# Moving the sums of w_down from the attention stage into the first MLP product of a two-layer f32 trunk

## The chip, the cores and the metric

The kernel runs on one core of a Trainium2 chip (trn2). The metric is the device time of one execution in microseconds (us), lower is better. The kernel before was timed three times: 2888.29, 2884.75 and 2887.67 us, median 2887.67.

The core has a matrix engine (PE, TensorE; PEld is its weight load), a vector engine (DVE, VectorE), a scalar engine (ACT, ScalarE), a general engine (POOL, GpSimd), and SP (SyncE), which here only issues DMA transfers. Each engine runs its own instructions strictly in the order in which they stand; an instruction that waits holds up everything behind it on its engine.

## The reference, cut to what matters

Two layers over 1088 tokens (1024 of a prompt, 64 of a sample), width 1024. Each layer is a mixer (layer 0: pooling and a recurrence, layer 1: windowed attention), then cross-attention into 256 memory tokens, then an MLP. All is f32. What the change touches is the MLP and the stage ahead of it:

```python
x = x + cross_attn(rmsnorm(x, p['norm_cross'][layer]), mem_k[layer], mem_v[layer],
                   p['w_mq'][layer], p['w_mo'][layer])
x = x + sq_relu_mlp(rmsnorm(x, p['norm_mlp'][layer]), p['w_up'][layer], p['w_down'][layer])
...
def sq_relu_mlp(h, w_up, w_down):        # w_up 1024 x 4096, w_down 4096 x 1024
    return jnp.square(jax.nn.relu(h @ w_up)) @ w_down
```

## The kernel before, in words

**Precision.** A f32 product is made of three matmuls: each operand is split into a rounded part (made by ACT) and the remainder (a subtraction on DVE), and low x high, high x low and high x high are added up in PSUM (`split`, L234, and `product`, L216). So every weight tile costs an ACT and a DVE instruction before PE can use it.

**Tokens** lie in two halves, s=0 (512) and s=1 (576); `x` holds the residual stream, features on partitions.

**The MLP by seven products.** Both MLP products are cut into 2 x 2 blocks and made with seven block products where eight are usual, with sums and differences of blocks as operands (the Strassen-Winograd scheme).
- The token operands B11, B12, B21, B22, T1 to T4 of a half are made by `operands` (L959): DVE scales x by the norm and gain (`scaled`), subtracts, and splits. For s=0 this runs under the last projection of cross-attention (`project_back`), for s=1 in one piece at slot 5 of the first MLP product (`hook`, L1192).
- The weight operands of w_up (A11, A12, A22, S1 to S4) are made per *stream*, which is 256 of the 4096 columns of w_up: two loads of 512 KB into `st` tiles by SP, four sums of 128x512 on POOL (L1050 to L1054, in `Up.weights`, L1036), seven splits (ACT L236, DVE L239 into `wp`).
- The first product, `Up.run` (L1077), runs 32 *rounds* of seven products (*slots*) each; a round is one stream with one token half, a product is 12 matmuls of 256 (s=0) or 288 (s=1) columns. Streams are mostly used for two rounds, s=0 and then s=1. The list of streams is 0, 1, 0, 2, 3, ..., 15, 14: streams 0 and 14 are loaded and made twice and used for one round each time. The numbers 5 and 7 in `self.at` say how many slots ahead of its use a weight operand may be made; it also has to wait until the operand of the stream before is used up.
- At the end of a round `finish` (L1094) takes relu and square of the result u on ACT, four sums of u on POOL (L1103 to L1106) into two single tiles `ss` and `sq`, and queues three stores to HBM, which SP issues at the fifth slot of the next round.
- The second product (`mlp_down`, L1218) loads quarters of w_down, or sums of its quarters, and the stored u and its sums.

**The sums of w_down** are made ahead of the MLP, under cross-attention: `weights_sums` (L937), called twice per head at L929, so 16 times per layer. Each call loads 1 MB of w_down into one tile `quarters` with two DMAs (SP, L942), makes four sums of 128x512 on POOL (L948) and stores the 1 MB with one DMA (SP, L949). The tile is single, so the next load waits for the store before it.

**Order.** A scheduler places most instructions; `keep_in_program_order` and `manual_schedule` pin some engines to the order of the program. In cross-attention the DMAs and POOL sums of `weights_sums` are pinned in that way; in the first MLP product SP, POOL and PE are. POOL also makes rc (the power -0.5 of the norm, L322) and the sum o (L908) in cross-attention, and issues the loads of keys and values (L792, L795).

Of the kernel before, what the change touches and what calls it, by code (L numbers as in the profile page):

```python
# [46 lines left out]
def body(ctx, tc, I, O):  # L47
# [7 lines left out]
    def f32(ap):  # L55
        return ap.bitcast(F32)
# [159 lines left out]
    def product(ps, small, big):  # L216
        terms = small + big
        for i, (a, b) in enumerate(terms):
            pe.matmul(ps, a, b, start=i == 0, stop=i == len(terms) - 1)  # L219
# [559 lines left out]
    def cross(l, s, norm, p, then):  # L779
# [135 lines left out]
        for j in range(4):  # L915
# [12 lines left out]
            for q in range(2):  # L928
                weights_sums(l, 8 * s + 2 * j + q, p)  # L929
# [6 lines left out]

    def weights_sums(l, q, p):  # L937

        a = p.tile([128, 4, 512], F32, tag="quarters", name="quarters", bufs=1)
        keep = tc.keep_in_program_order  # L940
        for i in range(2):
            keep(nc.sync.dma_start(a[:, 2 * i:2 * i + 2],  # L942
                                   I["w_down"][l][256 * q + 128 * i:256 * q + 128 * i + 128]
                                   .rearrange("p (h n) -> p h n", h=2)))

        for to, one, two, op in ((3, 1, 3, OP.add), (1, 0, 1, OP.subtract), (0, 3, 0, OP.subtract),
                                 (2, 2, 0, OP.subtract)):
            keep(pool.tensor_tensor(a[:, to], a[:, one], a[:, two], op))  # L948
        keep(nc.sync.dma_start(sums[l][q // 2][:, :, q % 2], a))  # L949
# [9 lines left out]
    def operands(s, g, nm, raw, ops, alloc):  # L959
# [14 lines left out]
        scaled(raw["B11"], 0, 0)  # L974
        yield
# [3 lines left out]
        parts("B11")  # L979
# [3 lines left out]
        scaled(raw["B21"], 4, 0)  # L983
        yield
        pool.tensor_tensor(raw["T3"], raw["B22"], raw["B12"], OP.subtract)
        dve.tensor_tensor(raw["T2"], raw["B22"], raw["T1"], OP.subtract)
        parts("T2")
        yield
        dve.tensor_tensor(raw["T4"], raw["T2"], raw["B21"], OP.subtract)
        for b in ("B21", "T1", "T4", "B22", "T3"):  # L990
            parts(b)
            yield
# [5 lines left out]
    class Up:  # L998


        def __init__(self, l):
            self.l = l
            self.streams = [0, 1, 0] + list(range(2, 16)) + [14]
            self.rounds = [(0, 0), (1, 0), (1, 1), (2, 1)]
            for k in range(3, 17):
                self.rounds += [(k, 0), (k, 1)] if self.streams[k] != 14 else [(k, 0)]
            self.rounds.append((17, 1))
# [14 lines left out]
            for w in range(count):  # L1022
                wanted = min(first[v] for v in range(w, min(w + 7, count))) - 5
# [12 lines left out]
        def weights(self, w):  # L1036
# [18 lines left out]
            elif name == "S3":  # L1055
                self.load(k + 1, 0)
                if k + 1 == len(self.streams):
                    W.resume(self.l, 2)
                    W.ahead()
# [17 lines left out]
        def run(self, ops, bufs, us, hook):  # L1077
# [16 lines left out]
            def finish(r):  # L1094
# [10 lines left out]
                pool.tensor_tensor(t[1], u[:, 2], t[0], OP.subtract)  # L1105
                pool.tensor_tensor(t[3], t[1], u[:, 1], OP.subtract)  # L1106
# [5 lines left out]
            store, sums_of_u = [], []  # L1112
            for i, (r, m) in enumerate(self.slots):
# [5 lines left out]
                cs.setdefault(r, bufs[r % 3])  # L1119
# [11 lines left out]
                product(ps, small, big)  # L1131
# [10 lines left out]
    def mlp(l, back, nm, last):  # L1142
# [18 lines left out]
        with phase(f"mlp{l}") as outer:  # L1161
# [29 lines left out]

            def hook(i):  # L1192
                r, m = up.slots[i]
# [6 lines left out]
                if r + 1 == len(up.rounds) and i % 7 == 0:  # L1200
# [522 lines left out]
```

## Time and profile before

| | |
|---|---|
| median of three runs | 2887.67 us |
| the profiled execution | 2890.01 us |
| its span, first to last instruction | 2888.2 us |
| PE busy | 2680.4 us (93%) |
| DVE / ACT / POOL busy | 1693.6 / 1247.5 / 772.2 us |
| cross-attention, layer 0 and 1 | 420 to 696 us, 1825 to 2110 us |
| first MLP product, layer 0 and 1 | 732 to 1113 us, 2147 to 2525 us |
| second MLP product, layer 0 and 1 | 1113 to 1454 us, 2525 to 2870 us |

PE is busy nearly all the time, so the time is the matmuls, the stretches in which PE stands still, and the stretches in which its granted clock is at the lower of its two levels (1.2 instead of 2.4 GHz, 0.5 in the records). A row of a timeline gives start, duration, engine, line, instruction, and in brackets how long the engine had been idle before it and what ended that.

### The profile page before, as it was taken

Reading aid. Unit: us, or ns where it says so; the run is one execution under the profiler, and the core shown is the slowest. Engines: PE = TensorE matmul, PEld = TensorE weight load, DVE = VectorE, ACT = ScalarE, POOL = GpSimd, SP = SyncE. Lnnn points to the kernel's source line nnn. Section 1 sums busy time; section 2 is a strip of 40 time slices with the busy share of each in tenths; the row PEclk is TensorE's granted clock in tenths of the full one; section 3 lists DMA queues with packets and bytes.
Section 4 is the critical chain, followed back from the end, with each engine's and each line's share of the span. In section 5 each row is a group of like instructions: output and inputs, shape, how many; then the busy total and the mean of one; then the engine's idle time right before and its main releaser. Section 6 shows DMA issues by size and latency. Waiting matters only on the chain. (4 is left out here: it accounts for less than half of the span.)

```text
span 2888.2 us, 47649 instructions
## 1 busy us (share of the span) xinstructions
PE 2680.4 (93%) x19048; PEld 2547.6 (88%) x19048; DVE 1693.6 (59%) x2844; ACT 1247.5 (43%) x2113; POOL 772.2 (27%) x762
## 2 busy tenths in 40 slices
PE   8999998878799999999999999987788999899998
PEld 7978997777799999999988899867688999899998
DVE  5595766556755556555458467655486545555454
ACT  5584644233434434333337356333334444433334
POOL 3200013333465552000003013243435555500000
PEclk9999999999899999999999999999899999999999
DMA  8722245654244447555340321456433444575552
GB/s 267 221 73 81 66 118 192 198 172 153 60 150 135 151 131 264 194 181 181 98 93 23 94 59 53 150 179 204 161 95 111 151 143 126 171 247 181 181 181 78
DMA packets 403938, 416.30 MB, mean 144 GB/s; under 512 B 48528, under 2 KB 335264, under 8 KB 403716
## 3 DMA queue, kind: packets, MB, share of 16 engines
q1 hardware_dynamic: 394820, 386.20, 42.1%
q0 software_dynamic: 8896, 27.06, 3.0%
q8 instruction: 149, 2.44, 0.4%
q14 instruction: 73, 0.60, 0.1%
HBM read 303.94 MB, written 109.39 MB: 143 GB/s over the span
## 5 line engine op out<-in xcount | busy, mean ns | idle before, releaser
L219 PE MATMUL mm<-hpH,wp 128*128 128x288 f32 (+3 forms) x3008 | 731.8, 330 | 42.4 <-DVE q L821 27.6
L219 PEld LDWEIGHTS mm<-hpH,wp 128*128 128x128 f32 x3008 | 518.8, 190 | 86.3 <-DVE q L821 29.8
L219 PE MATMUL mm<-hpL,wp 128*128 128x288 f32 (+3 forms) x1504 | 473.4, 330 | 2.3 <-DVE hpL L297 2.2
L185 ACT ACTIVATE wp<-st 128x1024 fp32r<-128x1024 f32 x218 | 229.5, 1056 | 361.0 <-PE mm L219 222.2
L239 DVE TENSOR_TENSOR wp<-st,wp 128x512 fp32r<-128x512 f32 x252 | 215.9, 865 | 251.4 <-ACT wp L236 249.3
L219 PE MATMUL s<-T,wp 128*128 128x288 f32 (+1 forms) x2304 | 312.5, 294 | 37.0 <-DVE wp L239 36.7
L186 DVE TENSOR_TENSOR wp<-st,wp 128x1024 fp32r<-128x1024 f32 x218 | 273.0, 1254 | 120.4 <-ACT wp L185 119.7
L219 PEld LDWEIGHTS s<-T,wp 128*128 128x128 f32 x2304 | 301.2, 193 | 42.5 <-DVE wp L239 42.0
L219 PEld LDWEIGHTS mm<-hpL,wp 128*128 128x128 f32 x1504 | 288.8, 192 | 21.4 <-DVE hpL L297 3.2
L948 POOL TENSOR_TENSOR quarters<-quarters 128x512 f32<-128x512 f32 x128 | 182.0, 1422 | 347.6 <-DMA quarters<-in_w_down_dram 340.2
L236 ACT ACTIVATE wp<-st 128x512 fp32r<-128x512 f32 x252 | 144.6, 621 | 267.1 <-POOL st L1052 208.4
L322 POOL TENSOR_TENSOR rc<-rc,mhalf 128x4 f32<-128x4 f32 (+1 forms) x21 | 22.4, 1076 | 850.4 <-DVE rc L321 850.4
L185 ACT ACTIVATE wd<-st 128x1024 fp32r<-128x1024 f32 x70 | 73.7, 1055 | 313.3 <-PE t L1259 299.9
L219 PE MATMUL mm<-B,wp 128*128 128x256 f32 (+1 forms) x1536 | 204.6, 288 | 4.1 <-DVE wp L239 4.1
L219 PEld LDWEIGHTS mm<-B,wp 128*128 128x128 f32 x1536 | 197.2, 188 | 5.3 <-DVE wp L239 5.3
L186 DVE TENSOR_TENSOR wd<-st,wd 128x1024 fp32r<-128x1024 f32 x70 | 86.3, 1236 | 158.7 <-ACT wd L185 158.7
L1257 PE MATMUL s<-uhl,wd 128*128 128x256 f32 x560 | 156.7, 284 | 9.5 <-ACT uhl L236 9.5
L1258 PE MATMUL s<-uhl,wd 128*128 128x256 f32 x560 | 157.4, 282 | 0.0
L1259 PE MATMUL s<-uhl,wd 128*128 128x256 f32 x560 | 156.9, 281 | 0.0
L239 DVE TENSOR_TENSOR uhl<-ur,uhl 128x1088 fp32r<-128x1088 f32 x112 | 143.9, 1286 | 17.8 <-ACT uhl L236 17.6
L236 ACT ACTIVATE uhl<-ur 128x1088 fp32r<-128x1088 f32 x112 | 123.4, 1104 | 49.0 <-DMA ur<-u 47.1
L1081 DVE TENSOR_TENSOR uC<-s,uC 128x256 f32<-128x256 f32 (+1 forms) x320 | 133.5, 432 | 11.6 <-PE s L219 5.0
(402 smaller groups left out, 6269.7 us busy)
## 6 DMA issues: line engine op xcount, KB each, us to landing
ur<-u SPq DMA_DIRECT2D x112, 544.0 KB, 6.0
st<-in_w_up_dram SPq DMA_DIRECT2D x72, 512.0 KB, 4.7
quarters<-in_w_down_dram SPq DMA_DIRECT2D x64, 512.0 KB, 4.7
sums<-quarters SPq DMA_DIRECT2D x32, 1024.0 KB, 5.7
st<-sums SPq DMA_DIRECT2D x64, 512.0 KB, 5.8
st<-in_w_down_dram SPq DMA_DIRECT2D x48, 512.0 KB, 5.0
st<-in_w_mq_dram SPq DMA_DIRECT2D x32, 512.0 KB, 4.5
st<-in_w_mo_dram SPq DMA_DIRECT2D x32, 512.0 KB, 6.9
```

What stands on the lines that cost most here:

```text
L185: act.activation(wt[:, 0], st, AF.Copy)
L186: dve.tensor_tensor(wt[:, 1], st, f32(wt[:, 0]), OP.subtract)
L219: pe.matmul(ps, a, b, start=i == 0, stop=i == len(terms) - 1)
L236: act.activation(h, src, AF.Copy)
L239: dve.tensor_tensor(l, src, f32(h), OP.subtract)
L322: pool.tensor_tensor(rc[:m, b0:b1], rc[:m, b0:b1], mhalf[:m, b0:b1], OP.pow)
L948: keep(pool.tensor_tensor(a[:, to], a[:, one], a[:, two], op))
L1081: dve.tensor_tensor(to, b, a, op)
L1257: pe.matmul(ps, wl, uh, start=first, stop=False)
L1258: pe.matmul(ps, wh, ul, start=False, stop=False)
L1259: pe.matmul(ps, wh, uh, start=False, stop=half == 1 and g == 3 and k == 1)
```

## The change

Four things are changed.
1. `weights_sums` leaves cross-attention and becomes a part of `Up.run`. There it handles 32 *pieces* per layer, half as large as before (256 of 512 columns), one per six slots from slot 24 on: two loads at turn 0, four POOL sums of 128x256 at turn 3, two stores at turn 5. All pieces use the same two tiles.
2. Two of the four sums of u go from POOL to DVE.
3. `operands` yields in smaller steps and in another order. For s=1 one step runs per slot from slot 5 on, instead of all at slot 5. The remainders of B22 and T3 are subtracted on POOL instead of DVE, for both halves.
4. The streams are 15, 0, 1, ..., 15 (17 instead of 18 are made; only the first and the last round use a stream alone), a weight operand may be made nine slots ahead instead of five, the matmuls of the very first product are pinned, and the pool of the second product opens one round earlier.

```diff
-            for q in range(2):
-                weights_sums(l, 8 * s + 2 * j + q, p)
...
-        def parts(b):
+        def parts(b, engine=dve):
             if b not in ops:
                 ops[b] = alloc(b)
-            split(ops[b][:, 0], ops[b][:, 1], raw[b])
+            act.activation(ops[b][:, 0], raw[b], AF.Copy)
+            engine.tensor_tensor(ops[b][:, 1], raw[b], f32(ops[b][:, 0]), OP.subtract)
...
-        for b in ("B21", "T1", "T4", "B22", "T3"):
-            parts(b)
-            yield
+        yield
+        parts("T4")
+        yield
+        parts("B22", pool)
+        parts("T3", pool)
...
-            self.streams = [0, 1, 0] + list(range(2, 16)) + [14]
...
+            self.streams = [15] + list(range(16))
+            self.rounds = [(0, 0)] + [(k, s) for k in range(1, 16) for s in range(2)] + [(16, 1)]
...
-                wanted = min(first[v] for v in range(w, min(w + 7, count))) - 5
+                wanted = min(first[v] for v in range(w, min(w + 7, count))) - 9
...
-                pool.tensor_tensor(t[1], u[:, 2], t[0], OP.subtract)
-                pool.tensor_tensor(t[3], t[1], u[:, 1], OP.subtract)
+                dve.tensor_tensor(t[1], u[:, 2], t[0], OP.subtract)
+                dve.tensor_tensor(t[3], t[1], u[:, 1], OP.subtract)
...
+            def weights_sums(i):
+
+                piece, turn = divmod(i, 6)
+                if i < 0 or piece >= 32:
+                    return
+                q, at = piece // 2, slice(256 * (piece % 2), 256 * (piece % 2) + 256)
+                if not quarters:
+                    quarters.extend(nrm.tile([128, NT2], F32, tag="rb", name="quarters", bufs=2)[:, :512]
+                                    .rearrange("p (h n) -> p h n", h=2) for _ in range(2))
+                (a11, a21), (a12, a22) = ((t[:, 0], t[:, 1]) for t in quarters)
+                if turn == 0:
+                    for j, t in enumerate(quarters):
+                        rows = I["w_down"][self.l][256 * q + 128 * j:256 * q + 128 * j + 128]
+                        nc.sync.dma_start(t, rows.rearrange("p (h n) -> p h n", h=2)[:, :, at])
+                elif turn == 3:
+                    pool.tensor_tensor(a22, a21, a22, OP.add)
+                    pool.tensor_tensor(a21, a11, a21, OP.subtract)
+                    pool.tensor_tensor(a11, a22, a11, OP.subtract)
+                    pool.tensor_tensor(a12, a12, a11, OP.subtract)
+                elif turn == 5:
+
+                    for j, t in enumerate(quarters):
+                        nc.sync.dma_start(sums[self.l][q // 2][:, 2 * j:2 * j + 2, q % 2, at], t)
...
+                weights_sums(i - 24)
...
-                    for _ in operands(1, g, nm1, raw1, ops[1], operand):
-                        pass
...
+                if 5 <= i < 24:
+                    next(make1, None)
```

On POOL, in the second token half of cross-attention of layer 0, these rows stand before the change (kvst are keys and values on their way in, o is a sum that the attention result waits for):

```order
L795 DMA kvst<-in_cache_mem_v_dram 128x2x256
L948 TENSOR_TENSOR quarters<-quarters 128x512 x4
L795 DMA kvst<-in_cache_mem_k_dram 128x2x256
L948 TENSOR_TENSOR quarters<-quarters 128x512 x4
L908 TENSOR_TENSOR o_5613<-o_5613 128x2x64
```

At the same place after the change:

```order
L797 DMA kvst<-in_cache_mem_v_dram 128x2x256
L797 DMA kvst<-in_cache_mem_k_dram 128x2x256
L910 TENSOR_TENSOR o_5533<-o_5533 128x2x64
L794 DMA kvst<-v_2_704 128x512
L794 DMA kvst<-kT_3_801 128x512
```

The sums of quarters are gone from between the loads and ahead of o.

On SP, in the middle of the first MLP product of layer 0, this stands before (u, ss and sq are the stores of one round, st the loads of w_up):

```order
L1122 DMA u_5_6354<-uC_6361 128x3x256
L1122 DMA u_5_6354<-ss 128x2x256
L1122 DMA u_5_6354<-sq 128x2x256
L1033 DMA st<-in_w_up_dram 128x8x128 x2
L1122 DMA u_5_6354<-uC 128x3x288
L1122 DMA u_5_6354<-ss 128x2x288
L1122 DMA u_5_6354<-sq 128x2x288
```

And this after:

```order
L1140 DMA u_5_6226<-uC_6233 128x3x256
L1140 DMA u_5_6226<-ss 128x2x256
L1140 DMA u_5_6226<-sq 128x2x256
L1025 DMA st<-in_w_up_dram 128x8x128 x2
L1130 DMA sums_5_89<-quarters 128x2x256 x2
L1121 DMA quarters<-in_w_down_dram 128x2x256 x2
L1140 DMA u_5_6226<-uC 128x3x288
L1140 DMA u_5_6226<-ss 128x2x288
L1140 DMA u_5_6226<-sq 128x2x288
```

The two stores of a piece and, directly behind them, the two loads of the next piece have come in; the stores wait for POOL's sums, the loads for the landing of the stores.

On DVE, where the token operands of s=1 of layer 0 are finished, this stands before (T and B are remainders of operands, rc and ra unsplit ones, wp a weight operand, uC the rounds' own sums):

```order
L986 TENSOR_TENSOR rc<-rb,rc 128x1152
L1081 TENSOR_TENSOR uC<-s,uC 128x256
L989 TENSOR_TENSOR ra<-rc,rb 128x1152
L239 TENSOR_TENSOR T_6904<-rc,T_6904 128x1152
L239 TENSOR_TENSOR B_6906<-rb,B_6906 128x1152
L239 TENSOR_TENSOR T_6905<-rc,T_6905 128x1152
L1090 TENSOR_TENSOR uC<-uC,t 128x256
L239 TENSOR_TENSOR wp<-st,wp 128x512
```

And this after:

```order
L975 TENSOR_TENSOR rc<-rb,rc 128x1152
L1074 TENSOR_TENSOR uC<-s,uC 128x256 x2
L1083 TENSOR_TENSOR uC<-uC,t 128x256
L1074 TENSOR_TENSOR uC<-s,uC 128x256
L959 TENSOR_TENSOR T_6780<-rc,T_6780 128x1152
L959 TENSOR_TENSOR T_6781<-rc,T_6781 128x1152
L982 TENSOR_TENSOR ra<-rc,rb 128x1152
L1098 TENSOR_TENSOR ss<-uC,ss 128x256
```

More of the rounds' own sums now stand between the operands, two of them (L1098, L1099) new on DVE.

## Rows read from the trace of the kernel before

**Rows 1.** The page's busy times of the whole span.
```profile
PE 2680.4 (93%) x19048; PEld 2547.6 (88%) x19048; DVE 1693.6 (59%) x2844; ACT 1247.5 (43%) x2113; POOL 772.2 (27%) x762
```
**Rows 2.** Stretches us: PE, PEld, DVE, ACT, POOL busy (count), clock, DMA share, GB/s.
```profile
420.00:696.00 276.00, 229.87 (x1336) 203.45 (x1335) 159.63 (x259) 100.28 (x210) 104.72 (x88) 0.93 0.57 183
732.40:1112.90 380.50, 349.08 (x2706) 345.08 (x2704) 213.64 (x382) 160.09 (x233) 209.96 (x196) 0.97 0.43 134
1825.00:2110.00 285.00, 235.55 (x1356) 207.63 (x1354) 162.35 (x261) 100.18 (x211) 105.80 (x88) 0.93 0.56 179
2146.60:2525.00 378.40, 351.20 (x2705) 347.22 (x2703) 214.96 (x382) 160.22 (x233) 206.25 (x196) 0.97 0.43 134
```
**Rows 3.** Waits of PE, 420 to 696 us: total us, times, longest us.
```profile
PE t L867 <- DVE pr L856: 18.9, 6, 10.5
PE t L332 <- POOL rc L322: 7.5, 1, 7.5
```
**Rows 4.** Timeline, 640 to 672 us: the longest stall of PE there.
```profile
660.26 5.28 POOL L948 TENSOR_TENSOR quarters<-quarters 128x512 f32<-128x512 f32 x4 [11.72 <-DMA quarters<-in_w_down_dram]
665.51 0.45 POOL L908 TENSOR_TENSOR o<-o 128x128 f32<-128x128 f32 x1
665.99 0.40 ACT L236 ACTIVATE hpH<-o 128x64 fp32r<-128x64 f32 x2 [10.81 <-POOL o L908]
668.64 1.09 PE L867 MATMUL t<-ident,pr 128*128 128x128 f32 x4 [10.47 <-DVE pr L856]
```
**Rows 5.** Timeline, 476 to 512 us: the stall at the norm.
```profile
495.90 5.28 POOL L948 TENSOR_TENSOR quarters<-quarters 128x512 f32<-128x512 f32 x4 [11.33 <-DMA quarters<-in_w_down_dram]
...
503.00 1.11 PE L332 MATMUL t<-ident,rc 128*128 128x128 f32 x4 [7.52 <-POOL rc L322]
```
**Rows 6.** Two calm stretches: early cross-attention, and two rounds of the first MLP product.
```profile
420.00:485.00 65.00, 62.51 (x329) 52.85 (x327) 50.90 (x70) 34.53 (x72) 24.65 (x21) 1.00 0.56 182
820.30:841.30 21.00, 21.00 (x169) 21.00 (x169) 11.12 (x21) 8.78 (x13) 12.34 (x13) 1.00 0.46 144
```
**Rows 7.** Timeline, PE alone, 796 to 806 and 1066 to 1084 us.
```profile
803.31 2.86 PE L219 MATMUL s<-T,wp 128*128 128x256 f32 x22 [1.69 <-DVE wp L239]
...
1069.46 3.09 PE L219 MATMUL mm<-B,wp 128*128 128x256 f32 x24 [1.35 <-DVE wp L239]
1076.41 6.03 PE L219 MATMUL s<-T,wp 128*128 128x256 f32 x36 [3.86 <-DVE wp L239]
```
**Rows 8.** Timeline, 735 to 772 us: token operands of the second half.
```profile
745.26 3.52 DVE L966 SCALAR_TENSOR_TENSOR ra<-x,gcol,rb 128x288 f32<-128x288 f32 x8 [1.41 <-ACT rb L333]
753.50 5.35 POOL L985 TENSOR_TENSOR uC<-rb,ra 128x1152 f32<-128x1152 f32 x1 [9.10 <-ACT uC L1084]
765.48 1.35 DVE L239 TENSOR_TENSOR T<-rc,T 128x1152 fp32r<-128x1152 f32 x1
767.82 2.93 PE L219 MATMUL s<-T,wp 128*128 128x256 f32 x12 [10.58 <-DVE wp L239]
```
**Rows 9.** POOL's groups, 809 to 1056 us: busy us, mean ns of one, idle before.
```profile
L1104 POOL TENSOR_TENSOR sq<-uC 128x288 f32<-128x288 f32 (+1 forms) x24 | 24.1, 1005 | 1.4 <-DMA u<-sq 1.4
L1106 POOL TENSOR_TENSOR sq<-ss,uC 128x288 f32<-128x288 f32 (+1 forms) x24 | 20.2, 844 | 1.9
L1050 POOL TENSOR_TENSOR st<-st 128x512 f32<-128x512 f32 x12 | 15.4, 1287 | 0.0
```
**Rows 10.** DMA issues, KB each and median us to landing: first MLP product, then cross-attention.
```profile
u<-ss SPq DMA_DIRECT2D x12, 256.0 KB, 2.2
...
quarters<-in_w_down_dram SPq DMA_DIRECT2D x32, 512.0 KB, 4.7
sums<-quarters SPq DMA_DIRECT2D x15, 1024.0 KB, 5.6
```
**Rows 11.** By tile, 809 to 1056 us: ns min/median/max of one instruction, for wp and ss.
```profile
L239 DVE TENSOR_TENSOR wp<-st,wp x80: 674/693/1234, 813.9 to 1053.3; 128x512 fp32r<-128x512 f32 x80
L1105 POOL TENSOR_TENSOR ss<-uC,ss x24: 733/814/1200, 809.3 to 1052.4; 128x288 f32<-128x288 f32 x12, 128x256 f32<-128x256 f32 x12
```

More of the change, by code (lines that the diff above doesn't have):

```diff
@@ L214, in body, with product @@
     W = Weights()
-    def product(ps, small, big):
+    def product(ps, small, big, in_order=False):
         terms = small + big
         for i, (a, b) in enumerate(terms):
-            pe.matmul(ps, a, b, start=i == 0, stop=i == len(terms) - 1)
+            m = pe.matmul(ps, a, b, start=i == 0, stop=i == len(terms) - 1)
+            if in_order:
+                tc.keep_in_program_order(m)
     def dense(ps, wt, c0, nk, rhs, order=None):
@@ L933, in cross @@
         return dict(s=s, key=("mo", l, s), pair=o, order=[range(6), range(6, 8)], spare=4 - 2 * s)
[L937 to L949, printed above, removed]
     def load_u(us, p, m, g):
@@ L978, in operands @@
         dve.tensor_tensor(raw["T1"], raw["B12"], raw["B11"], OP.subtract)
-        parts("B11")
         yield
@@ L982, in operands @@
         yield
[L983 removed]
+        dve.tensor_tensor(raw["T2"], raw["B22"], raw["T1"], OP.subtract)
+        pool.tensor_tensor(raw["T3"], raw["B22"], raw["B12"], OP.subtract)
         yield
[L985 to L986 removed]
         parts("T2")
         yield
+        parts("T1")
+        yield
         dve.tensor_tensor(raw["T4"], raw["T2"], raw["B21"], OP.subtract)
[L990 to L992 removed]
+        yield
+        parts("T4")
+        yield
+        parts("B22", pool)
+        parts("T3", pool)
     WT = dict(zip((1, 2, 3, 4, 5, 6, 7), ("A11", "A12", "S4", "A22", "S1", "S2", "S3")))
@@ L1002, in __init__ @@
             self.l = l
-            self.streams = [0, 1, 0] + list(range(2, 16)) + [14]
[L1004 to L1007, printed above, removed]
+            self.streams = [15] + list(range(16))
+            self.rounds = [(0, 0)] + [(k, s) for k in range(1, 16) for s in range(2)] + [(16, 1)]
             self.slots = []
@@ L1058, in weights @@
                     W.resume(self.l, 2)
-                    W.ahead()
+                    while W.load():
+                        pass
             elif name == "S4":
@@ L1112, in run @@
             store, sums_of_u = [], []
+            quarters = []
+            def weights_sums(i):
[19 more added lines that the diff above has]
+                        nc.sync.dma_start(sums[self.l][q // 2][:, 2 * j:2 * j + 2, q % 2, at], t)
             for i, (r, m) in enumerate(self.slots):
@@ L1130, in run @@
                     big.append((wh, b[:, 0, c]))
-                product(ps, small, big)
+                product(ps, small, big, i == 0)
                 for name, takes, make in flow:
@@ L1190, in mlp @@
             ready, pools = {}, {}
+            make1 = operands(1, g, nm1, raw1, ops[1], operand)
             def hook(i):
-                r, m = up.slots[i]
+                r, n = divmod(i, 7)
                 if i == 3:
@@ L1197, in hook @@
                     nm1.rows()
-                    for _ in operands(1, g, nm1, raw1, ops[1], operand):
-                        pass
-                if r + 1 == len(up.rounds) and i % 7 == 0:
+                if 5 <= i < 24:
+                    next(make1, None)
+                if r + 2 == len(up.rounds) and n == 0:
                     held.close()
@@ L1203, in hook @@
                     W.more = pools["down"]
-                if r + 1 == len(up.rounds) and 1 <= i % 7 <= 4:
-                    n = len(ready)
-                    ready[0, n] = load_u(us, pools["down"], 0, n)
+                if r + 1 == len(up.rounds) and n:
+                    W.ahead(min(n, 4))
+                    if n < 5:
+                        ready[0, n - 1] = load_u(us, pools["down"], 0, n - 1)
             with tc.manual_schedule(engines=engines):
```

9 lines of the change are left out of this document (5 added, 4 removed).

## The prediction

> **What bounds the kernel now.** I read the busy times first: PE 2680.4 us of the span [rows 1], so a gain can only come from the 208 us in which PE stands, or from stretches at its lower clock. The busy times by stretch say where these are (cross-attention and the first MLP product of layer 0, then of layer 1) [rows 2]. In cross-attention PE stands 276.0 - 229.9 = 46.1 us in layer 0 and 285.0 - 235.6 = 49.4 us in layer 1, together 95.5 us, and its mean granted clock is 0.93. In the first MLP product it stands 31.4 and 27.2 us at 0.97. Together that is most of what is to be had.
>
> The waits name DVE before most of the stalls in cross-attention [rows 3], but DVE is the messenger. The timeline shows the source: POOL stands 11.72 us for the transfer of `quarters`, makes its four sums in 5.28 us, and only then the 0.45 us sum o that stood behind them; ACT had waited 10.81 us for o, DVE behind ACT, and PE 10.47 us [rows 4]. At the norm the same: 11.33 us of waiting and 5.28 us of sums stand ahead of rc, and PE waits 7.52 us [rows 5]. So the sums of w_down cost nothing as work; they cost as a plug in POOL's queue, and by the pinned stores and loads in SP's.
>
> The first MLP product, undisturbed, takes 21.0 us for two rounds (169 matmuls) [rows 6], which is 1.50 us a slot and 9.0 us for the six slots of a piece. Its stalls are at the start (10.58 us [rows 8]) and where a stream used in one round only forces all weight operands to be renewed (1.69, 1.35 and 3.86 us in layer 0 [rows 7]).
>
> **The change part by part**, against the profiled execution of 2890.0 us.
>
> *Cross-attention loses the plug.* The standing is 95.5 us. The lost clock is 0.07 x 561 us = 39 us if it all fell on work and nothing if it all fell on standing; a low stretch covers the end of a stall and the work behind it, so I take half, 20. Total 115. What stays is bounded by the calm start of cross-attention, where PE stands 2.5 of 65 us with quarters already there [rows 6]: 3.8% of 561 us is 21 us; with a little clock I keep 25. Gain 90 (60 if DVE and ACT set half of the stalls themselves, 115 if nothing stays).
>
> *Streams.* The single-use turns at the second and the last but one stream go: 1.69 + 1.35 + 3.86 = 6.9 us per layer [rows 7], and I add an estimated 1.6 for low clock behind the longest; 17 for both layers. One set of weight operands and 1 MB of loads fewer hides under PE. The single use at both ends stays. Gain 17 (0 to 20).
>
> *Token operands in steps.* Before, DVE works through them in one go and a weight split waits behind them; PE stands 10.58 us [rows 8]. Now they are wanted from slot 14 on as before, but the work is the same: 16 scalings in 2 x 3.52, three subtractions and five remainders at 1.35, 17.9 us up to T4 [rows 8], and the rounds' own sums now stand between them, some 8 us more. From 745 that reaches 771, and slot 18, which needs T4, would come at 745 + 13 x 1.5 = 765: 6 us late. Then B22 and T3 leave DVE (1.35 each) for POOL, where the subtraction of the same size took 5.35 [rows 8], one after the other, since T3's operand takes the tile of unsplit B22: up to 10 us of which slots hide half. So 11 us against 10.58, and I take nothing for this part (10 us gained to 15 lost per layer).
>
> *Two sums of u on DVE.* POOL loses 64 x 0.92 us = 59 us per layer [rows 9]; DVE, busy 214 of 380 us [rows 2], takes them. POOL gains 128 quarter sums. No row has them in 128x256 with these operands; the nearest are u's sums at 0.92 (mean of two rows [rows 9]), 118 us. POOL goes from 210 to 269 of 380 us: not full. By work alone this costs nothing.
>
> *The pieces as a chain.* This is the cost. All pieces share two tiles, so each runs: loads, four sums, stores, and only then the next loads. SP, in order, holds the stores until POOL is done and the loads until the stores have landed; behind it stand the loads of w_up and the stores of u. POOL, in order, holds at the sums until the loads are in; behind them stand the sums of w_up's blocks, and PE waits for those. So if one turn of the chain takes more than the 9.0 us that PE gives it, PE is paced by the chain. One turn: a 256 KB store lands in 2.2 us [rows 10], two of them in some 2.7; two loads of 256 KB lie between that and the 4.7 of a 512 KB load of quarters, 3.6; four sums at 0.92 are 3.7. That is 10.0, 1.0 over, and with 32 pieces in 2 layers a loss of 64. The ends: 2.2 + 2.2 + 4 x 0.73 (the fastest such sum [rows 11]) = 7.3, nothing lost; and the 1 MB store and 512 KB loads, 5.6 + 4.7 + 4 x 1.2 = 15.1, 390 lost. I stay near the row of the same size, 256 KB. The first product's DMA share is 0.43 [rows 2] and the pieces add 32 x 2 x 0.52 = 34 MB per layer to 134 GB/s x 380 us = 51 MB, so their transfers will often meet others; that is why I take 3.6 and not 2.2 for the loads.
>
> The Trainium skill (DMA: Bandwidth & Descriptors, "Anatomy of one DMA") fits a transfer by 2.0 us and its bytes over 436 GB/s, about 2.6 us for 256 KB. By that the turn would be 2.6 + 2.6 + 3.7 = 8.9 and nothing would be lost; the row has 2.2 for such a store alone, and no row has one beside other transfers of this kind.
>
> Sum: 2890.0 - 90 - 17 + 64 = 2847. The profiled execution was 2.3 us over the median of the runs, so 2845.
>
> **The rivals.**
>
> *The chain fits (faster still).* If a turn stays at or under 9.0 us, the 64 goes: 2783, or 2781 against the median. For it: the 2.2 us of a 256 KB store, and that SP may issue loads ahead of the slot that needs them. Against it: POOL must also wait for each round's end.
>
> *The chain is too slow (slower).* The gains of 107 are used up at 107 / 64 = 1.7 us over, a turn of 10.7. At 12.0 the loss is 192 and the time 2973. For it: transfers that share the queues with 1 MB of u per round, quarters that took 4.7 us, and u's sums on POOL that reach 1.2 [rows 11]. Against it: when PE is paced, the other transfers and POOL's other work thin out too.
>
> *The engines' access to memory is the bound, not the chain.* Beside the chain, POOL's sums and DVE's two-input subtractions disturb each other: the split of a weight takes 0.67 us at best and up to 1.23, a sum of u 0.73 and up to 1.20 [rows 11]. If of the two only one can run at a time, two rounds need on POOL 9.3 quarter sums x 0.73, 4 sums of w_up x 1.29 [rows 9] and 4 sums of u x 0.73 = 14.9 us, and on DVE 7 splits x 0.67 and 4 sums of u at about half of that = 6.1; together 21.0 of 21.0 us. With a tenth unusable that is 23.3, 2.3 us over in 32 pairs of rounds, 74: 2890 - 107 + 74 = 2857, 2855 against the median. The Trainium skill (SBUF — State Buffer, "Who interferes with whom") has this as an exclusive lock between a DVE instruction with two inputs in SBUF and a GpSimd instruction that reads it. The longest of these rows agree, the medians (0.69 and 0.81) show that they seldom met so far.
>
> *Cross-attention keeps its stalls* (DVE or ACT is late without POOL too), and the chain takes what the streams give: 2885, no change. Against it: in both stalls shown POOL ends last.
>
> **How the numbers follow.** The forecast 0.40 (own range 2815 to 2875), the chain fits 0.24, the access bound 0.10, stalls kept 0.06, the chain too slow 0.20. The first three are faster by over 0.2% (5.8 us, about what a measurement of this kernel tells from no change): 0.74; no change 0.06; slower 0.20. The range runs from 2775, just under the time of the fitting chain, to 2925, which leaves out the worse half and more of the slow chain.
>
> **What would show it.** Right: in cross-attention the stalls before L867 and L332 fall under 3 us and the granted clock rises to 0.98; in the first MLP product PE waits for weight operands every few rounds, POOL for quarters several us per piece, and rounds of 10 and 11 us grow to 11 and 12. Wrong: rounds at the pace of before (the chain fits), or stretches of the first MLP product of over 430 us (too slow); cross-attention stalls of over 5 us with POOL idle; a start of the first product without a long stall, which would make the operand steps worth 10 us per layer.

## The result, and the profile after

The changed kernel takes 2937.34 us (median, 2935.89 to 2939.19) against 2886.45 us of the kernel before on the same chip: ratio 1.0177, 95% interval 1.0159 to 1.0194. It is slower by 51 us, and the prediction had the sign wrong. The page's busy times and the four stretches of [rows 2] (us, then busy us and count of PE, PEld, DVE, ACT and POOL, then clock, DMA share, GB/s) show both halves of it:

```profile
PE 2707.2 (92%) x19048; PEld 2570.1 (88%) x19048; DVE 1730.5 (59%) x2950; ACT 1237.9 (42%) x2099; POOL 697.4 (24%) x762
```
```profile
426.60:677.10 250.50, 246.73 (x1565) 224.89 (x1564) 165.09 (x289) 114.79 (x229) 31.57 (x31) 1.00 0.27 79
677.10:1141.20 464.10, 376.97 (x2704) 365.66 (x2703) 254.47 (x434) 156.18 (x226) 255.60 (x260) 0.92 0.57 180
1860.80:2111.00 250.20, 246.47 (x1564) 224.93 (x1563) 165.12 (x289) 113.40 (x228) 31.64 (x31) 1.00 0.27 79
2111.00:2573.90 462.90, 376.66 (x2706) 365.02 (x2704) 254.25 (x435) 156.27 (x226) 255.97 (x260) 0.92 0.57 180
```

Cross-attention, from the first score product to the first MLP product, takes 250.5 us where the same 1564 matmuls took 309.5 (422.9 to 732.4, the row below), in layer 1 250.2 where they took 314.4: 123 us gained. PE stands 3.8 us there in each layer, against 49.8 and 53.6, and the clock is at full speed.

```profile
422.90:732.40 309.50, 259.74 (x1564) 233.10 (x1563) 187.72 (x291) 115.49 (x229) 114.79 (x93) 0.93 0.54 172
```

The first MLP product goes from 380.5 to 464.1 and from 378.4 to 462.9 us: 168 us lost. Of the 83.6 us in layer 0, 55.7 are standing (87.1 against 31.4) and 27.9 are the same matmuls taking longer, 376.97 us where they took 349.08 [rows 2], because the granted clock falls to its lower level behind some of the stalls: it is 0.50 from 896 to 899 us, around the end of the first stall shown below.

The waits of PE in the first MLP product of layer 0 (total us, times, longest) name DVE's splits of w_up, and the timeline of PE shows the pattern:

```profile
PE s L219 <- DVE wp L241: 35.6, 21, 6.0
PE t L219 <- DVE wp L241: 24.8, 8, 3.9
```
```profile
897.92 5.93 PE L219 MATMUL s<-T,wp 128*128 128x256 f32 x36 [5.96 <-DVE wp L241]
...
920.01 1.68 PE L219 MATMUL t<-T,wp 128*128 128x256 f32 x12 [3.65 <-DVE wp L241]
...
948.66 2.75 PE L219 MATMUL t<-T,wp 128*128 128x256 f32 x12 [3.87 <-DVE wp L241]
...
983.02 6.04 PE L219 MATMUL s<-T,wp 128*128 128x256 f32 x36 [5.24 <-DVE wp L241]
```

From 897.92 to 983.02 is 85.1 us for 42 slots, seven pieces: 12.2 us a piece, where PE alone needs 9.0. In the same stretch the chain of pieces stands in POOL's timeline as follows:

```profile
904.90 0.95 POOL L1123 TENSOR_TENSOR quarters<-quarters 128x256 f32<-128x256 f32 x1
...
914.55 0.74 POOL L1123 TENSOR_TENSOR quarters<-quarters 128x256 f32<-128x256 f32 x1 [6.16 <-DMA quarters<-in_w_down_dram]
...
917.65 0.72 POOL L1096 TENSOR_TENSOR ss<-uC 128x256 f32<-128x256 f32 x1
...
920.04 1.41 POOL L1042 TENSOR_TENSOR st<-st 128x512 f32<-128x512 f32 x1 [0.96 <-DVE wp L241]
...
924.80 0.74 POOL L1123 TENSOR_TENSOR quarters<-quarters 128x256 f32<-128x256 f32 x1
...
943.21 0.74 POOL L1123 TENSOR_TENSOR quarters<-quarters 128x256 f32<-128x256 f32 x1 [8.15 <-DMA quarters<-in_w_down_dram]
```

The turns are 9.65, 10.25 and then 18.4 us; the next four are 10.21, 10.43, 10.05 and 16.1. Of the 22.1 us by which these seven are over 9.0 each, the two long ones hold 16.5. What the 18.4 is made of stands in the timeline of SP's queue:

```profile
921.69 1.84 SPq L1140 DMA_DIRECT2D u<-sq  x1
929.40 2.88 SPq L1025 DMA_DIRECT2D st<-in_w_up_dram  x2
932.33 1.09 SPq L1130 DMA_DIRECT2D sums<-quarters  x2
937.65 1.20 SPq L1121 DMA_DIRECT2D quarters<-in_w_down_dram  x2
```

POOL had the sums ready at 928.8, but SP stood from 923.5 to 929.4 before a load of w_up (L1025) whose buffer DVE had not yet given back, and the store of the piece stood behind it until 932.3; the next load then waited for that store to land, 937.65. The turn of 16.1 us is made of places in POOL's order instead:

```profile
973.90 0.81 POOL L1123 TENSOR_TENSOR quarters<-quarters 128x256 f32<-128x256 f32 x1 [2.57 <-DMA quarters<-in_w_down_dram]
...
977.12 1.27 POOL L1042 TENSOR_TENSOR st<-st 128x512 f32<-128x512 f32 x1
...
988.47 0.81 POOL L1096 TENSOR_TENSOR ss<-uC 128x288 f32<-128x288 f32 x1 [6.06 <-ACT uC L1095]
...
990.00 0.95 POOL L1123 TENSOR_TENSOR quarters<-quarters 128x256 f32<-128x256 f32 x1
```

A piece's sums stood ahead of the sums of w_up, so PE stood 5.24 us before 983.02; the next piece's sums stood behind the sums of u, which waited for the end of that late round. SP's and POOL's waits of the whole stage:

```profile
SPq L1025 <- DVE wp L241: 113.4, 22, 18.3
SPq L1130 <- POOL quarters L1125: 105.3, 27, 5.9
SPq L1121 <- DMA sums<-quarters: 49.7, 41, 4.2
```
```profile
POOL quarters L1123 <- DMA quarters<-in_w_down_dram: 78.1, 19, 8.2
```

The kernel before had SP standing at the same loads already (its waits of SP, 800 to 1040 us). There the pieces' stores and loads were not yet behind them:

```profile
SPq L1033 <- DVE wp L239: 103.6, 23, 8.2
```

### The profile page after: what moved, and what is told of

Same layout as the page of the kernel before. It is cut to its first block, busy times and chain, and to the rows that moved or that the text cites. A ratio compares the mean times of both kernels' runs of the same rounds, so it can differ in the third digit from the quotient of the medians.

```text
span 2934.1 us, 48032 instructions
## 1 busy us (share of the span) xinstructions
PE 2707.2 (92%) x19048; PEld 2570.1 (88%) x19048; DVE 1730.5 (59%) x2950; ACT 1237.9 (42%) x2099; POOL 697.4 (24%) x762
## 5 line engine op out<-in xcount | busy, mean ns | idle before, releaser
L219 PE MATMUL s<-T,wp 128*128 128x256 f32 (+1 forms) x2304 | 333.1, 305 | 73.0 <-DVE wp L241 58.1
L219 PEld LDWEIGHTS s<-T,wp 128*128 128x128 f32 x2304 | 318.1, 203 | 82.9 <-DVE wp L241 66.4
L185 ACT ACTIVATE wp<-st 128x1024 fp32r<-128x1024 f32 x218 | 229.8, 1056 | 373.7 <-PE mm L219 270.0
L238 ACT ACTIVATE wp<-st 128x512 fp32r<-128x512 f32 x238 | 138.4, 622 | 425.5 <-POOL st L1044 290.2
L219 PE MATMUL mm<-B,wp 128*128 128x256 f32 (+1 forms) x1536 | 215.4, 298 | 5.5 <-DVE wp L241 5.4
L219 PEld LDWEIGHTS mm<-B,wp 128*128 128x128 f32 x1536 | 207.2, 198 | 8.7 <-DVE wp L241 8.6
L1098 DVE TENSOR_TENSOR ss<-uC,ss 128x288 f32<-128x288 f32 (+1 forms) x64 | 62.6, 977 | 257.4 <-POOL ss L1096 257.4
L219 PE MATMUL t<-T,wp 128*128 128x256 f32 (+1 forms) x768 | 120.6, 311 | 50.2 <-DVE wp L241 48.6
L219 PEld LDWEIGHTS t<-T,wp 128*128 128x128 f32 x768 | 111.5, 210 | 54.4 <-DVE wp L241 52.3
```

The lines of the kernel that those rows point to most:

```text
L185: act.activation(wt[:, 0], st, AF.Copy)
L219: m = pe.matmul(ps, a, b, start=i == 0, stop=i == len(terms) - 1)
L238: act.activation(h, src, AF.Copy)
L1098: dve.tensor_tensor(t[1], u[:, 2], t[0], OP.subtract)
```

## The experiments

Theory A: the turn of a piece on one pair of tiles is too long. B: the sums of u on DVE tie the splits to POOL. C: POOL's time, or the access to memory of the prediction's third rival. F came later: the place of a piece in POOL's order. Kernels that leave sums out say so in their expectation. Timed beside them, the kernel before took 2885.1 to 2887.8 us (medians), which says how far small differences can be read.

**e1, sums of u back on POOL.**
```diff
-                dve.tensor_tensor(t[1], u[:, 2], t[0], OP.subtract)
-                dve.tensor_tensor(t[3], t[1], u[:, 1], OP.subtract)
+                pool.tensor_tensor(t[1], u[:, 2], t[0], OP.subtract)
+                pool.tensor_tensor(t[3], t[1], u[:, 1], OP.subtract)
```


> The changed kernel (2937 us) with the last two of the four sums of u given back to POOL, nothing else. Theory B (the sums on DVE tie DVE's queue, and with it the splits of w_up, to a POOL that stands before quarters still on their way: 257 us of waits at L1098): the waits of PE for DVE's splits at the first product of a round (2.3 to 3.9 us each) go, 2860 to 2895 us. Theory A (the chain load, four sums, store on two tiles is slower than its six slots, and POOL's own sums of w_up stand behind it): the chain still sets the pace and POOL has about 1.5 us more work in each round, 2930 to 2965 us.

Measured 2940.6 us, the same. DVE's waits at these sums were real (81.0 us of 240), but with POOL plugged they only move. B falls as the main cause.

**e2, no pieces.** The call `weights_sums(i - 24)` goes, and the plan reads quarters:
```diff
-                    src = sums[l][g][:, q]
+                    src = dram(w, (4 * g + q // 2) * 128 * D + q % 2 * 512, [[D, 128], [256 * D, 2], [1, 512]])
```


> The changed kernel without the sums of w_down: no loads, sums and stores of pieces in the first MLP product, and the second one reads quarters of w_down itself in their place, so its output isn't the reference's. Theories A and B alike: all that the first product lost was the pieces; its stages fall from 464 and 463 us to 360 to 375 us each, 2740 to 2770 us in all. Theory D (the operands in steps, or the new order of rounds, cost time themselves): the stages stay above 395 us each, 2800 us or more.

Measured 2769.3 us: the pieces cost 168.0 us, all that the first product lost (its stages are 380.6 and 380.5 us).

**e3, half of the pieces.**
```diff
-                piece, turn = divmod(i, 6)
+                piece, turn = divmod(i, 12)
```


> The changed kernel with half of the pieces, one in twelve products in place of one in six (the other half of the sums isn't made, and the second product reads quarters of w_down itself there, so its output isn't the reference's). Theory A: a turn of 10 to 12 us fits into twelve slots of 18 us, so the loss is not halved but all but gone: within 15 us of the kernel without pieces. Theory C (every piece costs the same by the port that POOL and DVE share, or by DMA traffic): half of what the pieces cost stays, about 85 us above the kernel without pieces.

Measured 2810.4 us, 41 above no pieces: a quarter of the cost for half of the pieces. Neither theory's number: a turn of 18 us is long enough for the chain, yet each piece still costs 1.3 us (2.6 at the full rate).

**e4, the kernel before without its sums.** The two calls in cross-attention go, the plan as in e2.

> The kernel before, with the sums of w_down left out of the cross-attentions and made nowhere (the second product reads quarters of w_down itself, so its output isn't the reference's): what the sums cost where they stood. By the stalls that went in the changed kernel, 59 and 64 us in the two cross-attentions: 2755 to 2775 us against 2886. By the 90 us of the prediction: 2797 us.

Measured 2755.7 us: where they stood, the sums cost 130.5 us. In cross-attention of layer 0 PE stands 0.5 us without them:

```profile
423.10:670.00 246.90, 246.36 (x1564) 224.76 (x1563) 164.30 (x291) 114.82 (x229) 22.93 (x29) 1.00 0.28 80
```

**e5 and e6, the sums alone and the transfers alone.** In e5 the loads run once and the stores go; in e6 the four `pool.tensor_tensor` of turn 3 go.

> The changed kernel with the four POOL sums of every piece at their places, but without the pieces' transfers: one pair of quarters is loaded once for each layer and nothing is stored (the second product reads quarters of w_down itself, so its output isn't the reference's). Theory A (what costs is the turn: sums that wait for loads, loads that wait for stores, stores that stand in SP's queue behind loads of w_up): the waits go, 2770 to 2795 us against 2769 without pieces and 2937 with them. Theory C (POOL's time and the port that it shares with DVE): 128 sums in each layer cost by themselves, 2830 us or more.

> The changed kernel with the loads and stores of every piece at their places, but without the four POOL sums between them (so what is stored are the quarters themselves and its output isn't the reference's). Theory A: load and store alone take 3.5 + 2.2 us and some issues of a turn of 9.0 us, and no POOL instruction waits for them, so PE stalls only where SP holds up the loads of w_up: 2775 to 2815 us. If the traffic itself costs (256 KB transfers in the way of the loads of w_up): 2850 us or more.

Measured 2831.6 and 2846.0 us, 62 and 77 above no pieces. The first lies in C's range, the second between its two. A alone falls: sums without any transfer cost too. In e5's timeline of POOL, then ACT, another reason than C stands in order of time:

```profile
865.10 0.94 POOL L1123 TENSOR_TENSOR quarters<-quarters 128x256 f32<-128x256 f32 x1
...
868.14 1.07 POOL L1126 TENSOR_TENSOR quarters<-quarters 128x256 f32<-128x256 f32 x1
869.17 1.75 POOL L1042 TENSOR_TENSOR st<-st 128x512 f32<-128x512 f32 x1
...
872.35 1.26 POOL L1044 TENSOR_TENSOR st<-st 128x512 f32<-128x512 f32 x1
```
```profile
873.64 2.19 ACT L238 ACTIVATE wp<-st 128x512 fp32r<-128x512 f32 x4 [8.14 <-POOL st L1044]
```

The piece's four sums take POOL from 865.1 to 869.2, right ahead of the sums of w_up (L1042 to L1044) on which the next split waits; PE then stood 3.80 us before 875.56. Since pieces come every six products and a stream has fourteen, this meeting returns every 42 products. In e6 no sum waits, but the stores of u stand in SP's queue behind those of the pieces, and POOL's first sum of u, which reuses their tile, waits for them (waits of POOL, 800 to 1040 us):

```profile
POOL ss L1096 <- DMA u<-ss: 80.9, 9, 11.1
```

**e7, stores issued by POOL.** `nc.sync` becomes `pool` at turn 5.

> The changed kernel with the stores of the pieces issued by POOL right behind its sums in place of SP. In the changed kernel's trace three turns in four take some 10 us, and the fourth 18.4 us because the store stands in SP's queue behind a load of w_up that waits for its buffer. If that queue is half of the loss (theory A, SP's part): the long turns go, a turn is 9.7 to 10.3 us against 9.0, the stages of the first product fall from 464 to 400 to 425 us, 2815 to 2865 us in all. If the chain's own length is all of it: 2920 us or more, since POOL's issues come on top.

Measured 3016.6 us, 79 slower than the changed kernel: A's range is missed, and the other case gave only a lower bound. The stores now stand in POOL's order, some behind sums of w_up, and each issue takes POOL 0.73 us; which of the two costs more wasn't separated. Another in-order queue was no way out here.

**e8, the kernel before with the sums apart.** `pieces` replaces `weights_sums`; every call does three steps of three different pieces:
```diff
+                for j, t in enumerate(held.pop(i - 2)):
+                    keep(nc.sync.dma_start(sums[l][q // 2][:, 2 * j:2 * j + 2, q % 2, at], t))
...
+                    keep(pool.tensor_tensor(to, one, two, op))
...
+                held[i] = [p.tile([128, 2, 256], F32, tag=f"quarters{j}", name="quarters", bufs=3) for j in range(2)]
```


> The kernel before with its sums of w_down left in the cross-attention, but in pieces of 256 columns on three pairs of tiles: each call stores the piece before last, sums the last one and loads a new one, 34 calls spread over both passes and the output projection between them, so that POOL and SP find what they need. If what the sums cost there (130 us, by the kernel before without them) is waiting in order and not traffic or POOL's time: 2760 to 2800 us, and the fastest complete kernel so far. If it is traffic or the port: 2840 us or more.

Measured 2797.5 us, as expected (ratio 0.9686, 0.9669 to 0.9703): of the 130.5 us that the same sums cost in the same stage, 42 stay. Three things differ at once: the three pairs, the half-size pieces, and their spread over more of the stage. Cross-attention of layer 0, now with DMA share 0.65 and PE standing 12.4 us:

```profile
423.50:688.00 264.50, 252.09 (x1565) 228.36 (x1564) 186.27 (x291) 114.98 (x229) 135.81 (x154) 0.98 0.65 200
```

**e9, loads of w_up later.** `load` is put off by four slots.

> The changed kernel, complete, with each load of w_up put into SP's queue four products (6 us) later than now. In the trace of the changed kernel SP stands 39.8 us of 240 before these loads until a split on DVE sets their buffer free, up to 6.4 us at a time, and the stores and loads of the pieces stand behind them. If that is what makes the turns of a piece 12.1 us on average where the chain alone takes 10: the turns fall to 10 to 10.5 us, the stages of the first product from 464 to 405 to 430 us, 2815 to 2870 us in all. If SP's order is no part of it: 2925 us or more.

Measured 2919.9 us, just under the second case: 17 of the 168 go. SP's waits from 800 to 1040 us, the changed kernel's line first, then two of this run (L1026 loads w_up, L1137 stores a piece):

```profile
SPq L1025 <- DVE wp L241: 39.8, 12, 6.4
```
```profile
SPq L1137 <- POOL quarters L1132: 79.5, 18, 9.5
SPq L1026 <- DVE wp L241: 1.7, 5, 0.4
```

SP's stand before these loads is all but gone from there, and yet most of the cost stays: SP now stands 79.5 us before POOL's sums (61.9 in the changed kernel). So that stand is a part, not the main one.

**e10 and e11, the other parts without pieces.** e10 is e4 with the changed `Up.__init__`, rounds and hook, but operands and sums of u as before; e11 is e2 with the edit of e1.

> The kernel before without its sums of w_down (2755.7 us; the second product reads quarters of w_down itself, so the output isn't the reference's), with the change's order of streams and rounds and its earlier splits alone: the second half's operands are made at one place as before, the four sums of u stand on POOL. By the prediction's 17 us for the streams: 2739 us. If the streams gain nothing: 2752 to 2760 us. If they are what makes the changed kernel without pieces 13.6 us slower than this: 2769 us.

> The changed kernel without the pieces (2769 us, its output isn't the reference's for the same reason) with all four sums of u on POOL. If the two sums on DVE cost nothing, as predicted: 2767 to 2771 us. If they are part of the 13.6 us by which it is slower than the kernel before without sums: 2756 to 2764 us. What remains between this and the run with the streams alone is the operands made step by step.

Measured 2740.5 and 2754.4 us. The streams gain 15.2, the operands in steps cost 13.9, the two sums on DVE 14.9. The waits in e2, first MLP product of layer 0, show where the last stands: with POOL free of pieces, DVE still stands at its sum until POOL has made the one before, and PE stands 10.4 us for splits, where in e11 (the last line) it is 4.0:

```profile
DVE ss L1098 <- POOL ss L1096: 83.4, 31, 3.1
PE s L219 <- DVE wp L241: 10.4, 11, 2.8
```
```profile
PE s L219 <- DVE wp L241: 4.0, 6, 2.1
```

The stage takes 380.6 us, in e11 373.8. A split on DVE also takes 999 ns on average in e2 and 873 in e11, so how much of the 7 us is the wait and how much the longer splits isn't separated.

**e12, layer 1's sums in layer 0's second MLP product.** As e8 for layer 0; for layer 1 one pair of tiles, loads on SP, sums and stores on POOL.

> The kernel before, complete, with layer 0's sums of w_down in pieces spread over the cross-attention as in the run with the sums apart, and layer 1's in layer 0's second MLP product, where POOL is busy for under 5 of 341 us: load on SP, sums and store on POOL, one pair of tiles, a piece every 10 us. The first cost 17.6 us there, the second 21.3 us in cross-attention 1. If a stage whose POOL is idle takes them for nothing: 2770 to 2783 us. If the transfers (32 MB in 341 us) hold up the second product's loads: 2797 us or more.

Measured 2854.8 us, the second case by its bound: the second product of layer 0 grows from 342 to 416 us. POOL was idle there, but the loads on SP now wait for the stores of the one pair, with the loads of u behind them (waits of SP, 1072 to 1487 us; L969 loads a piece):

```profile
SPq L969 <- DMA sums<-quarters: 260.1, 39, 10.0
```

**e13 and e14, fixed places.** 26 pieces per layer at two places of every 14 products; e13 the sums alone, e14 complete, with the other six pieces in cross-attention.
```diff
+                for odd, load, add, save in ((0, 0, 1, 2), (1, 3, 4, 9)):
+                    turn = (i - 33) % 14
```


> The changed kernel with the pieces' POOL sums alone (no transfers of pieces; the second product reads quarters of w_down itself, so the output isn't the reference's), as in the run with the sums alone (2832 us, 62 above no pieces), but 26 pieces in each layer at two fixed places of every 14 products: right behind POOL's sums of w_up, and right behind the next sums of u. Theory F (a piece costs only where its place, which moves through the rounds since six and seven don't divide, comes ahead of the sums of w_up on POOL): 2769 to 2788 us. If POOL's time itself costs: 62 x 26/32 = 50 us above 2769, 2819 us.

> The changed kernel, complete, with 26 of the 32 pieces of each layer at these fixed places, their stores behind the loads of w_up on SP, and the other six spread over the cross-attention. Theory F, and SP's order with it: 2775 to 2825 us (2769 without pieces, some 7 us for six pieces in each cross-attention, the rest for SP). If the turn of a piece (10 us alone) is what decides whatever the place: 26/32 of 168 us above 2769, 2905 us.

e13: 2788.5 us, 19 above no pieces where 50 would be its share of 62: for the sums alone F holds. C doesn't explain it: a piece's four sums take longer here than in e5 (3.7 us on average, there 3.45), and cost less. e14: 2905.3 us, F and SP's order miss by 80, and the other case, that the turn of a piece decides whatever its place, had 2905. By an estimate (136 us above no pieces, less 8 for the twelve pieces in cross-attention by e8) a piece at a fixed place still costs 2.5 us, against 2.6. In e14's timelines of SP and POOL a period is (L1051 loads w_up, L1148 and L1156 load and store a piece, L1150 is its first sum, L1122 the sum of u):

```profile
897.38 1.48 SPq L1051 DMA_DIRECT2D st<-in_w_up_dram  x2
898.96 1.51 SPq L1156 DMA_DIRECT2D sums<-quarters  x2
905.18 1.21 SPq L1148 DMA_DIRECT2D quarters<-in_w_down_dram  x2
```
```profile
909.49 0.73 POOL L1150 TENSOR_TENSOR quarters<-quarters 128x256 f32<-128x256 f32 x1 [7.76 <-DMA quarters<-in_w_down_dram]
...
912.61 0.72 POOL L1122 TENSOR_TENSOR ss<-uC 128x256 f32<-128x256 f32 x1
```

The load waits for the store on the same tiles (900.5 to 905.2), POOL for the load, the sum of u and DVE behind POOL; PE stood 3.31 us before 914.97.

**e15, the last with the sums of u and the operands as before.**

> The last kernel with the two other parts that cost time undone: all four sums of u on POOL (14.9 us by the runs without pieces) and the second half's operands made at one place (13.9 us). If the parts add up: 29 us below the last kernel. If POOL's two more sums in each round fill the room that the pieces use: 10 us below it or less.

Measured 2885.4 us, 20 below e14: between the two expectations.

**e16, the streams and the sums apart.** e8 and e10 together, complete.

> Complete: the change's streams alone (2740.5 us without sums), and all of w_down's sums in the cross-attentions in pieces spread over three pairs of tiles (42 us in the kernel before). If the parts add up: 2782 us, below the kernel before with the sums apart (2797.5 us) by the streams' 15 us.

Measured 2782.2 us, ratio 0.9645 (0.9627 to 0.9663): the parts add up, and this beats both kernels.

**e17, three pairs of tiles, and e18, that with the loads of w_up later.**
```diff
-                piece, turn = divmod(i, 6)
+                turn, rest = divmod(i, 3)
...
+                    return n // 4, slice(128 * (n % 4), 128 * (n % 4) + 128), quarters[2 * (n % 3):2 * (n % 3) + 2]
```


> The changed kernel, complete, with pieces half as wide (128 columns, 64 in each layer, one in three products) on three pairs of tiles: every turn stores the piece before last, sums the last one and loads a new one, so no load waits for the store of the piece just made, and no sum for a load just issued. As many bytes, twice the transfers. Theory A (one pair of tiles: the load waits for the store, and POOL, and w_up's sums behind it, for the load): the waits of POOL for quarters go and the cost of the pieces falls from 168 us to what the sums alone cost by their place, some 60 us, 2825 to 2860 us. If the transfers themselves are the cost (77 us alone) or SP's queue: 2890 us or more.

> The same with the loads of w_up four products later in SP's queue, so that stores and loads of the pieces stand less behind them. If SP's stand before the loads of w_up is what is left: 20 us or more below the last kernel. If the three pairs have given the pieces room enough to bear it, or the sums' place is what is left: within 8 us of it.

e17: 2867.9 us (ratio 0.9930, 0.9914 to 0.9947). The cost of the pieces falls from 168 to 98.5, though they are now twice as many transfers; 8 us over A's range. In its waits of SP (800 to 1040 us; L1125 stores a piece) those for a store that has to land are down from 32.4 to 1.2 us. POOL's waits for loads of quarters don't go, as A expected, but halve (50.7 us in the changed kernel):

```profile
SPq L1025 <- DVE wp L241: 50.9, 13, 6.8
SPq L1125 <- POOL quarters L1130: 24.0, 13, 3.6
```
```profile
POOL quarters L1128 <- DMA quarters<-in_w_down_dram: 26.1, 21, 2.5
```

e18: 2893.3 us, 25 slower, a miss. What gave 17 in e9 costs 25 here, though SP's stand before the loads of w_up falls from 50.9 to 2.9 us (800 to 1040 us). In the same stretch a new wait stands on POOL, for the store of the sum of u before; that it is the cause wasn't tested:

```profile
POOL ss L1103 <- DMA u<-ss: 21.7, 6, 5.5
```

## Why the prediction was wrong

| step | predicted us | measured us | by |
|---|---|---|---|
| cross-attention loses the plug | -90 | -130.5 | e4 against before (2886.2) |
| streams | -17 | -15.2 | e10 against e4 |
| token operands in steps | 0 | +13.9 | e11 against e10 |
| two sums of u on DVE | 0 | +14.9 | e2 against e11 |
| the pieces (predicted as a chain) | +64 | +168.0 | after against e2 |
| sum | -43 | +51 | |

The step that failed is the chain's, "That is 10.0, 1.0 over, and with 32 pieces in 2 layers a loss of 64." The turn itself was right: five of the seven turns measured take 9.65 to 10.43 us, and loads of 256 KB 3.5 us (predicted 3.6). Wrong was that a stage pays only the excess of the chain's own turn over 9.0 us: the other two turns take 16.1 and 18.4 us and hold three quarters of the loss in that stretch. The chain doesn't run by itself. Three things were left out:

- The piece's sums stand ahead of the sums of w_up on POOL at some places of the 42-product cycle, which costs without any transfer: 62 us (e5), 19 with 26 of 32 pieces at fixed places (e13). With the transfers, fixed places gained little (e14). The prediction had named what stands behind POOL, but let it pay only when the chain is late.
- Every store and load of a piece stands in SP's queue behind loads of w_up. The trace before had SP standing 103.6 of 240 us there, a row that the prediction's working left out. It makes the 18.4 us turn shown; but with that stand gone from the middle of the stage only 17 us went (e9), and with three pairs of tiles taking it away cost 25 (e18).
- Each late turn closes a loop, as the timelines read: load waits for store, POOL for load, sums of u and w_up behind POOL, the splits on DVE behind those, PE behind the splits, and SP's loads of w_up again behind the splits. With three pairs of tiles the first link is cut, and 69 of 168 us go (e17), the most that one kernel took away. Its pieces are also half as wide and stand at other places, so not all of the 69 is shown to be that link's.

And a third of the loss is no standing at all: 27.9 of 83.6 us in layer 0 are matmuls at the lower clock, which the term for the chain didn't hold.

Two costed at nothing were not. "By work alone this costs nothing" was true of the work: DVE had room. But the moved sums take their input from POOL's and stand in DVE's queue ahead of splits, so DVE waits 83.4 us in a stage (e2); some 7 us in each stage come of the move. The operands in steps have their cost in two places: at the end of the output projection, where two products wait 3.4 us in each layer for DVE's additions to x (0.2 in e10), and in the first product, 4.1 and 2.7 us (e11's stages against e10's). Together some 7 us per layer, they lie in the bounds given (15 us lost per layer); for the sums of u none were given.

The gain in cross-attention was under-sized by 40: I had let 25 us of standing and clock remain and counted half of the clock; in e4 0.5 us and a clock of 1.00 are left.

Of the rivals, *the chain is too slow* came true, by its sign, its place and its signature (stretches of over 430 us; an average turn of 12.2 us against the 12.0 that it had priced at 2973). Not by its reasons, though, which were slower transfers and sums: loads and stores took what the forecast gave them, and the average comes of two long turns in seven. Its time was 36 us too high: 40 more were gained in cross-attention and the chain lost 168 instead of 192, against 29 for the two parts costed at nothing. *The access bound* isn't what decided between places: sums of a piece take longer in e13 than in e5 and cost less. The Trainium skill (SBUF — State Buffer, "Who interferes with whom") has the lock between the two engines; the trace agrees in that a quarter sum of 0.74 us takes 1.07 beside a split in e5. The fit of the Trainium skill (DMA: Bandwidth & Descriptors, "Anatomy of one DMA") that the prediction sets against its turn is made there for transfers that GpSimd issues; SP issues these.

Not settled: what of the 69 us is the link, the width and the place (e17); of the 98.5 us left with three pairs some 62 may be the sums' places (e5), but that sum wasn't tried with that width; the 77 us of the transfers alone have a wait that fits (u's stores behind the pieces' in SP's queue), not an experiment that takes it away; why e18 is slower is open.

## What to carry to other kernels

Work that is free as work is not free as a place in an in-order queue: before moving it, list for each queue it enters what already waits there, and what stands behind the new entry, and read the queue's own waits in the stage that receives it. A chain load, compute, store on one pair of tiles wants each step in another turn, on three pairs, so that no step waits for the one just issued; with half-size pieces spread over more of the stage, that made the same sums cost 42 us where they had cost 130 (e8). A fixed place in the period of the work around it helped sums alone (e13), not a chain on one pair of tiles (e14). And measure a piece of a change that you would cost at zero by itself.

## What the runs showed that was not expected

- Halving a transfer didn't shorten it: pieces of 256 KB land in 2.2 (store) and 3.5 us (load) in the changed kernel, of 128 KB in 3.3 and 3.1 us in e17. A transfer of 128 columns has as many rows as one of 256, each half as long, and the DMA share from 800 to 1040 us is 0.70 there against 0.61; which of these holds the time up wasn't tested. The fit of the Trainium skill (DMA: Bandwidth & Descriptors, "Anatomy of one DMA"), made there for transfers that GpSimd issues, gives an estimated 2.6 and 2.3 us; no run shows the smaller one at that beside the other transfers of this stage.
- Half-size sums on POOL aren't half as long: 0.46 us for 128x128 in e17 and 0.74 for 128x256 in the changed kernel (medians).
- A transfer issued by POOL takes 0.73 us of POOL's own time (e7), 1.5 us for the two stores of a piece.
